# Second-layer projections of a two-layer streaming encoder: the two value products moved among the query products, the sink terms loaded earlier

## The chip, the cores and the metric

The kernel runs on one core of one Trainium2 chip. The metric is the device time of one execution in microseconds (us), given as the median of several runs. The engines are named as in the profile: PE (TensorE), DVE (VectorE), ACT (ScalarE), POOL (GpSimd) and SP (SyncE, whose queue issues all the DMAs of this kernel).

## The reference, cut to what matters

One step of a hybrid encoder on a prompt of 4096 tokens and a sample of 64 tokens, model width 1024. Layer 0 is a gated convolution module. Keys and values come from one shared projection behind it, and layer 1 reads them in a windowed attention with one learned sink per head.

```python
def trunk(x, conv_hist, k_prefix, v_prefix):
    ...
    x, h = conformer_conv_layer(x, conv_hist[i], a_pre_g[i], ...)   # layer 0
    kv = rmsnorm(x, kv_g) @ w_kv                  # 1024 x 256: keys | values
    ...
    x = swa_layer(x, ctx, b_pre_g[j], b_w_in[j], b_sinks[j], b_w_out[j], b_post_g[j])

def swa_layer(x, ctx, pre_g, w_in, sinks, w_out, post_g):
    h = rmsnorm(x, pre_g)
    z = h @ w_in                                  # 1024 x 2048: query | gate
    q, gate = jnp.split(z, 2, axis=-1)
    o = sink_alibi_attention(q, kb, vb, q_pos, k_pos, sinks)
    y = (o * jax.nn.silu(gate)) @ w_out
    return x + rmsnorm(y, post_g)

def sink_alibi_attention(q, k, v, q_pos, k_pos, sinks):
    ...
    sink = sinks.reshape(N_KV_HEADS, GROUP)[None, None, :, :, None, None]
    m = jnp.maximum(jnp.max(s, axis=-1, keepdims=True), sink)
    p = jnp.exp(s - m)
    denom = jnp.sum(p, axis=-1, keepdims=True) + jnp.exp(sink - m)
```

## The kernel before

The program has three stages in the order of time: layer 0 (0 to some 1550 us of the trace), the second layer's projections (some 1550 to 1996 us), and attention with gate and output projection (to the end at 2940 us). The change touches a load that belongs to the third stage and the order of work in the second.

**The projection stage** goes through 16 blocks of 256 prompt tokens, and through the sample. A block has two tiles of 128 tokens. `load_x1` (L1038 to L1048) reads the rows of layer 0 back from DRAM, four DMAs of 128 KB per tile (L1046), two tiles ahead of their use. `prep_x1` normalises: per tile four ACT squares with sums (L1063), one matmul `tot` that adds them over partitions (L1068), a reciprocal root (DVE L1070, POOL L1073), four scaled copies into PSUM (ACT L1085, `pst_b`), four DVE transposes (L1089), and the split of the result in two fp16 halves, `hTb` (ACT L1091 high, DVE L1092 low). From both tiles come the sums that a Strassen product needs, `tf` (POOL L1119 to L1127), split in the same way into `tTb` (ACT L1103, DVE L1104). `hTb` and `tTb` are stored to DRAM (L1135, L1137) for the gate of the third stage.

`proj_qkv` (L1170 to L1260) lists the products of one block. Each full product is three fp16 passes. The query projection is one level of Strassen (L990 to L1032): seven products p1, p5, p6, p2, p7, p4, p3, each 48 matmuls (L983), into three PSUM tiles: `sx_q` holds p1, p6, p7 and p4 in turn and is copied out by ACT between them (L1001, `P_q`, `U_q`), `sz_q` holds p5 and then p3, `sw_q` holds p2. Behind p7, DVE adds `sz_q` into the copied tile (L1256, `U_q<-sz_q,U_q`), and p3 goes on in the same `sz_q`, so p3 has to wait for that add. `k_job` is one key product (`psk`, 24 matmuls, L189 to L191), `v_job(0)` and `v_job(1)` are the value products of the two tiles (`psv`, 24 matmuls each), drained by ACT (L1185) and DVE (L1186) into `vo`. Queries are drained likewise (ACT L1231, DVE L1232, `q`).

`sz_q` and both `psv` come from one PSUM pool of two buffers. `sz_q` is held from p5 to the end of p3's drain, so while a block is between p5 and p3 its two value products share the one other buffer: the second waits until the first is drained.

**What sets the order.** The code appends work as closures, and a scheduler fixes each engine's instruction order when the program is built, from its own estimate of times. The list that `proj_qkv` returns (L1260) is what the change rewrites; the order on all engines around it follows from it. In eight of the blocks a step of preparing the gate's weights runs as well (`strassen_chunk`, L924 to L975: eight loads `wst` at L934, ACT L943, POOL L953, casts L960 and L961); these are called gated blocks here, the others plain blocks. Gated blocks fill some 1657 to 1874 us.

**The sink terms.** `sk` (L1375 to L1378) holds the 16 sinks on all partitions: two DMAs that each write 64 partitions times 8 elements of 4 bytes, from a rearranged source that is repeated over the partitions. `nsk` (eight DVE multiplies, L1382) and `unsc` (eight POOL memsets, L1383) are made from it or beside it, and the attention reads them after 2000 us. In this order of the program `sk` is loaded behind the convolution weights' close (`main_w.close()`), at the start of the projection stage.

Of the kernel before, what the change touches and what calls it, by code (L numbers as in the profile page):

```python
# [12 lines left out]
F32 = mybir.dt.float32  # L13
# [5 lines left out]
P = 128  # L19
# [48 lines left out]
def tile_streaming_conformer(  # L68
# [5 lines left out]
    nc = tc.nc  # L74
# [8 lines left out]
    cpool = ctx.enter_context(tc.tile_pool(name="const", bufs=1))  # L83
# [9 lines left out]
    def ps_cv(shape, name):  # L93
        return pcv["pool"].tile(shape, F32, tag="cv", name=name)
# [82 lines left out]
    def mm3(out, wts, mov, low_last=False):  # L177
        n = len(wts)
        if low_last:
            for i in range(n):  # L180
                nc.tensor.matmul(out, wts[i][0], mov[i][0], start=i == 0, stop=False)  # L181
                nc.tensor.matmul(out, wts[i][0], mov[i][1], start=False, stop=False)  # L182
            for i in range(n):
                nc.tensor.matmul(out, wts[i][1], mov[i][0], start=False, stop=i == n - 1)  # L184
            return
        for i in range(n):
            wh, wl = wts[i]
            mh, ml = mov[i]
            nc.tensor.matmul(out, wh, mh, start=i == 0, stop=False)  # L189
            nc.tensor.matmul(out, wh, ml, start=False, stop=False)  # L190
            nc.tensor.matmul(out, wl, mh, start=False, stop=i == n - 1)  # L191
# [27 lines left out]
    def big(shape, dt, name):  # L219
        return wk.tile(shape, dt, tag="big", name=name, bufs=6)  # L220
# [687 lines left out]
    for g in range(1, 4):  # L908
        nc.gpsimd.tensor_copy(fv[:, g], fv[:, 0])

    gq = cpool.tile([P, 4, KB], F32, name="gq")
    for j in range(4):
        nc.gpsimd.tensor_scalar(gq[:, j], gsc[:, 2], scalar1=2.0**j, scalar2=None, op0=ALU.mult)
# [76 lines left out]
    def strassen(w, h, t, tmp, out, nm):  # L990
        def bl(kh, th):
            return lambda z, kb: h[z][:, KH * kh + kb, th * P : th * P + P]

        def tl(x):
            return lambda z, kb: t[z][:, x, kb, :]

        X = {}

        def cp(name, src):
            X[name] = tmp(f"{name}_{nm}", name)  # L1000
            nc.scalar.copy(X[name], src)  # L1001

        def p1():
            X["X"] = ps_mm([P, KH, P], f"sx_{nm}")
            sprod(X["X"], w["A11"], bl(0, 0), True, False)
            cp("P1", X["X"])

        def p5():
            X["Z"] = ps_cz([P, KH, P], f"sz_{nm}")
            sprod(X["Z"], w["S1"], tl(0), True, False)  # L1010

        def p6():
            sprod(X["X"], w["S2"], tl(1), False, False)
            cp("U2", X["X"])

        def p2():
            X["W"] = ps_mm([P, KH, P], f"sw_{nm}")
            sprod(X["W"], w["A12"], bl(1, 0), True, True)
            out(0, 0, X["W"], X["P1"])

        def p7():
            sprod(X["X"], w["S3"], tl(2), False, False)
            cp("U3", X["X"])
            out(1, 1, X["Z"], X["U3"])

        def p4():
            sprod(X["X"], w["A22"], tl(3), False, True)
            out(1, 0, X["X"], None)

        def p3():  # L1030
            sprod(X["Z"], w["S4"], bl(1, 1), False, True)
            out(0, 1, X["Z"], X["U2"])  # L1032

        return [p1, p5, p6, p2, p7, p4, p3]
# [135 lines left out]
    def proj_qkv(b, ht, pool):  # L1170
# [12 lines left out]
        def put_v(src, n, scale, dst, name):  # L1183
            o = pool.tile([P, 2, P], F16, tag="vo", name=name)
            nc.scalar.activation(o[:n, 0], src, AF.Copy, scale=scale)  # L1185
            nc.vector.scalar_tensor_tensor(  # L1186
                out=o[:n, 1], in0=src, scalar=scale, in1=o[:n, 0], op0=ALU.mult, op1=ALU.subtract
            )
            nc.sync.dma_start(out=dst, in_=o[:n])
# [16 lines left out]
        def v_job(i):  # L1206
            n = min(P, T - i * P)
            last = samp or t0 + i * P + n == SEQ
            ps = ps_cv([P, 2 * P], f"psv_{b}_{i}")
            wts = [(hT[0][:, kb, i * P : i * P + n], hT[1][:, kb, i * P : i * P + n]) for kb in range(KB)]  # L1210
            lo = 0 if last else P
            mv = [(w_kv.at(0, kb, lo, 2 * P - lo), w_kv.at(1, kb, lo, 2 * P - lo)) for kb in range(KB)]
            mm3(ps[:n, lo : 2 * P], wts, mv)
            put_v(ps[:n, P:], n, SX / SP, v_scs[WIN:] if samp else v_scr[t0 + i * P : t0 + i * P + n], f"vo_{b}_{i}")
            if last:
                kv = big([P, D], F32, f"kvo_{b}")
                nc.scalar.activation(kv[:n, : 2 * P], ps[:n], AF.Copy, scale=1.0 / SP)
                for c, dst in ((0, ck_s if samp else ck_p), (P, cvv_s if samp else cvv_p)):
                    nc.sync.dma_start(
                        out=dst[0, WIN - n : WIN].rearrange("t k d -> t (k d)"), in_=kv[:n, c : c + P]  # L1220
                    )
# [35 lines left out]
            put_q(nh, th, src)  # L1257

        q = strassen(wq, hT, tT, tmp, out, f"q{b}")
        return [q[0], q[1], k_job, q[2], q[3], q[4], lambda: v_job(0), q[5], lambda: v_job(1), q[6]]  # L1260

    hts = {}
    with ExitStack() as ph:
# [48 lines left out]
    stp = ctx.enter_context(tc.tile_pool(name="stp", bufs=1))  # L1312
# [59 lines left out]

    bias = stp.tile([P, 3 * CH], F32, tag="bias", name="bias", bufs=1)
    nc.sync.dma_start(out=bias, in_=ins["alibi"])
    sk = stp.tile([P, 2, 4], F32, tag="sk", name="sk", bufs=1)  # L1375
    sinks = ins["b_sinks"][0].rearrange("(a t s) -> s a t", a=2, s=2)
    for s_ in range(2):
        nc.sync.dma_start(out=sk[s_ * 64 : s_ * 64 + 64], in_=sinks[s_].partition_broadcast(64))  # L1378
    nsk = stp.tile([P, 2, 4], F32, tag="nsk", name="nsk", bufs=1)
    unsc = stp.tile([P, 2, 4], F32, tag="unsc", name="unsc", bufs=1)  # L1380
    for t in range(8):
        nc.vector.tensor_scalar_mul(nsk[:, t // 4, t % 4 : t % 4 + 1], sk[:, t // 4, t % 4 : t % 4 + 1], -SQ * 2.0**t)  # L1382
        nc.gpsimd.memset(unsc[:, t // 4, t % 4 : t % 4 + 1], 2.0**-t / SQ)  # L1383
# [54 lines left out]
    with ExitStack() as ph:  # L1438
# [29 lines left out]
        for q_, b in enumerate(order3):  # L1468
            jobs = deque(proj_qkv(b, hts[b], p3))
            if q_ > 0 and q_ + 1 < nb:  # L1470
                b2 = order3[q_ + 1]
                hts[b2], steps = prep_x1(b2, x1n.pop(0))
                nxt.extend(steps)
            n = max(1, len(jobs))
            per = -(-len(nxt) // n)
            while jobs:
                jobs.popleft()()
                for _ in range(per):
                    if nxt:
                        nxt.popleft()()  # L1480
            while nxt:
                nxt.popleft()()
            if q_ + 2 < nb:
                x1n.append(load_x1(order3[q_ + 2]))
            while wnext:
                with queued():
                    wnext.pop()()
            for js, at in ((ojobs, 0), (gjobs, G_AT)):
                if js and q_ >= at:
                    load, comp = js.popleft()  # L1490
                    load()
                    wnext.append(comp)
            if q_ == nb - 2:
                load_att(0)
                gate_load(0)
# [315 lines left out]
```

## Time and profile before

| | us |
|---|---|
| median of 3 runs | 2932.94 |
| range of the runs | 2931.07 to 2938.25 |
| the profiled execution | 2942.24 |
| its span, first to last instruction | 2940.2 |
| PE busy in the span | 2777.6 |
| DVE busy in the span | 2263.9 |
| a plain block (1632.04 to 1656.89) | 24.85 |
| gated blocks, mean of eight (1656.89 to 1873.82) | 27.1 |

The profiled execution is 9.3 us above the median of the runs, and 2.0 us of its time lie outside the span. An engine's busy time is the sum of its instructions' durations. A row of a timeline gives an instruction's start, its duration, the engine, the line and the tiles, and in brackets how long the engine had been idle before it and what released it. A block's time is counted here from the second value product of one block to that of the next.

### The profile page before, as it was taken

What the parts mean: (1) busy time and instruction counts of PE and PEld (TensorE: products, weight loads), DVE (VectorE), ACT (ScalarE), POOL (GpSimd) and SP (SyncE); (2) the same over time, 40 slices, a digit from 0 to 9 for tenths busy, and PEclk for the clock granted to TensorE, in tenths of its full rate; (3) what the DMA queues carried; (4) which work ended last, traced back from release to release, by engine and by line L of the source; (5) the groups of instructions that cost most, each with busy time, mean ns of one, the idle gap of its engine ahead of it and who ended that gap; (6) DMA issues with size and microseconds to landing.
All of it is one profiled execution on the core that took longest, in us unless ns stands there. A gap on an engine that the chain in (4) does not pass through costs nothing. (4 is left out here: it accounts for less than half of the span.)

```text
span 2940.2 us, 62260 instructions
## 1 busy us (share of the span) xinstructions
PE 2777.6 (94%) x24441; PEld 1803.0 (61%) x24441; DVE 2263.9 (77%) x3828; ACT 1785.4 (61%) x3957; POOL 1689.9 (57%) x1614
## 2 busy tenths in 40 slices
PE   7988999999999997989998999998999999999998
PEld 5433454444444443444448999997777777777775
DVE  5899888989888889978885777754667766666665
ACT  5666667666765565556675777743565565556554
POOL 4888578779876798887752343323333343433432
PEclk9999999999999998999999999999999999999999
DMA  5121111121120124656655656666233422332321
GB/s 165 55 79 68 52 54 49 38 71 44 50 74 34 39 70 133 204 170 199 190 181 173 218 201 214 220 210 203 78 101 95 145 93 93 118 123 84 113 79 60
DMA packets 256011, 341.16 MB, mean 116 GB/s; under 512 B 40070, under 2 KB 184198, under 8 KB 254950
## 3 DMA queue, kind: packets, MB, share of 16 engines
q1 hardware_dynamic: 255717, 337.20, 35.7%
q8 instruction: 191, 3.13, 0.4%
q14 instruction: 103, 0.84, 0.1%
HBM read 206.46 MB, written 130.72 MB: 115 GB/s over the span
## 5 line engine op out<-in xcount | busy, mean ns | idle before, releaser
L622 DVE SCALAR_TENSOR_TENSOR acc<-u,pt,acc 128x1024 f32<-128x1024 f32 x608 | 782.3, 1287 | 63.7 <-ACT acc L615 49.7
L606 POOL TENSOR_TENSOR pacc<-pacc,prods 128x1024 f32<-128x1024 f32 x213 | 506.2, 2378 | 114.9 <-ACT prods L597 82.3
L597 ACT ACTIVATE prods<-u,pt 128x1024 f32<-128x1024 f32 x213 | 242.2, 1145 | 95.2 <-POOL pacc L606 94.4
L1567 ACT ACTIVATE p<-p,st 128x192 f32<-128x192 f32 (+1 forms) x520 | 228.8, 443 | 90.9 <-DVE st L1561 86.5
L606 POOL TENSOR_TENSOR pacc<-pacc,pr 128x1024 f32<-128x1024 f32 x107 | 254.4, 2378 | 39.6 <-ACT pr L597 34.7
L1540 DVE CUSTOM_DVE_ANT_0 p<-sc,bias 128x192 f32<-128x192 f32 (+1 forms) x520 | 159.6, 350 | 82.0 <-PE sc L1537 59.4
L1586 POOL TENSOR_TENSOR p<-p,st 128x768 f32<-128x768 f32 (+2 forms) x130 | 189.8, 1480 | 37.9 <-DVE st L1582 35.8
L181 PE MATMUL psy<-w_oa,hl 128*128 128x512 f16 x512 | 199.4, 389 | 10.5 <-ACT hl L307 9.2
L189 PE MATMUL ps_gt<-hT,w_gt 128*128 128x512 f16 x512 | 196.0, 383 | 10.1 <-ACT w_gt L160 5.2
L182 PE MATMUL psy<-w_oa,hl 128*128 128x512 f16 x512 | 198.8, 388 | 3.3 <-DVE w_oa L161 3.3
L189 PE MATMUL ps_a<-hT,w_a 128*128 128x512 f16 (+1 forms) x528 | 198.6, 376 | 3.0 <-ACT sig L785 1.9
L191 PE MATMUL ps_a<-hT,w_a 128*128 128x512 f16 (+1 forms) x528 | 198.4, 376 | 3.2 <-DVE w_a L161 3.1
L189 PE MATMUL ps_gl<-hT,w_gl 128*128 128x512 f16 (+1 forms) x528 | 198.4, 376 | 1.9 <-ACT sig L785 1.2
L181 PE MATMUL psy<-w_ob,ogT 128*128 128x512 f16 x512 | 194.1, 379 | 5.0 <-ACT ogT L1652 5.0
L190 PE MATMUL ps_gl<-hT,w_gl 128*128 128x512 f16 (+1 forms) x528 | 197.7, 375 | 0.8 <-DVE hT L208 0.8
L190 PE MATMUL ps_a<-hT,w_a 128*128 128x512 f16 (+1 forms) x528 | 198.4, 376 | 0.0
L191 PE MATMUL ps_gl<-hT,w_gl 128*128 128x512 f16 (+1 forms) x528 | 197.9, 375 | 0.0
L191 PE MATMUL ps_gt<-hT,w_gt 128*128 128x512 f16 x512 | 195.2, 382 | 2.7 <-DVE w_gt L161 2.7
L190 PE MATMUL ps_gt<-hT,w_gt 128*128 128x512 f16 x512 | 196.1, 383 | 0.0
L182 PE MATMUL psy<-w_ob,ogT 128*128 128x512 f16 x512 | 194.1, 379 | 0.0
L983 PEld LDWEIGHTS <-w_qS 128*128 128x128 f16 x3072 | 180.1, 100 | 11.3 <-issue 10.9
L983 PEld LDWEIGHTS <-w_gS 128*128 128x128 f16 x3072 | 180.5, 98 | 8.7 <-issue 6.9
(363 smaller groups left out, 7171.7 us busy)
## 6 DMA issues: line engine op xcount, KB each, us to landing
x<-in_x_prompt SPq DMA_DIRECT2D x32, 512.0 KB, 3.4
g_scr<-sg SPq DMA_DIRECT2D x64, 256.0 KB, 2.0
c_scr<-c SPq DMA_DIRECT2D x32, 512.0 KB, 2.6
c<-c_scr SPq DMA_DIRECT2D x32, 512.0 KB, 5.7
g<-g_scr SPq DMA_DIRECT2D x32, 512.0 KB, 4.3
x<-x_scr SPq DMA_DIRECT2D x128, 128.0 KB, 3.7
h_scr<-hTb SPq DMA_DIRECT2D x32, 512.0 KB, 3.4
h_scr<-tTb SPq DMA_DIRECT2D x32, 512.0 KB, 4.8
```

What stands on the lines that cost most here:

```text
L181: nc.tensor.matmul(out, wts[i][0], mov[i][0], start=i == 0, stop=False)
L182: nc.tensor.matmul(out, wts[i][0], mov[i][1], start=False, stop=False)
L189: nc.tensor.matmul(out, wh, mh, start=i == 0, stop=False)
L190: nc.tensor.matmul(out, wh, ml, start=False, stop=False)
L191: nc.tensor.matmul(out, wl, mh, start=False, stop=i == n - 1)
L597: nc.scalar.activation(dst[:, :T], u[:, k : k + T], AF.Identity, scale=wdw[:, j, k : k + 1], bias=pt[:, j, R_DWB : R_DWB + 1] if k == 0 el ...
L606: nc.gpsimd.tensor_tensor(out=pacc[:, :T], in0=pacc[:, :T], in1=dst[:, :T], op=ALU.add)
L622: nc.vector.scalar_tensor_tensor(out=acc[:, :T], in0=u[:, k : k + T], scalar=wdw[:, j, k : k + 1], in1=acc[:, :T], op0=ALU.mult, op1=ALU.add,)
L983: nc.tensor.matmul(ps[:, j, :], w[:, wz, kb, j * P : j * P + P], rhs(rz, kb), start=first and j + kb + wz + rz == 0, stop=last and j == KH ...
L1540: nc.vector.tensor_tensor_reduce(out=pbuf[:, t, par * 192 + lo : par * 192 + 192], in0=ps[:, tt, :nk], in1=bias[:, lo:], scale=1.0, scalar ...
L1567: nc.scalar.activation(pp, pp, AF.Exp, scale=2.0 ** -(kv * 4 + t) / SQ, bias=st[:, 1, par, t : t + 1], accum_out=st[:, 3, par, t : t + 1],)
L1586: nc.gpsimd.tensor_tensor(out=pp, in0=pp, in1=st[:, 4, par, :, None].to_broadcast([P, 4, 3 * CH - lo]), op=ALU.mult)
```

## The change

The list of `proj_qkv` is reordered: the two value products, which stood behind p7 and p4, now stand behind p1 and behind p6, with the key product between them. The tile `sk` moves to the pool of constants and its two DMAs are issued in the code of the setup ahead of layer 0; `nsk` and `unsc` move to the same pool.

```diff
@@ -908,6 +908,10 @@
+    sk = cpool.tile([P, 2, 4], F32, name="sk")
+    sinks = ins["b_sinks"][0].rearrange("(a t s) -> s a t", a=2, s=2)
+    for s_ in range(2):
+        nc.sync.dma_start(out=sk[s_ * 64 : s_ * 64 + 64], in_=sinks[s_].partition_broadcast(64))
@@ -1257,7 +1261,7 @@
         q = strassen(wq, hT, tT, tmp, out, f"q{b}")
-        return [q[0], q[1], k_job, q[2], q[3], q[4], lambda: v_job(0), q[5], lambda: v_job(1), q[6]]
+        return [q[0], lambda: v_job(0), q[1], k_job, q[2], lambda: v_job(1), q[3], q[4], q[5], q[6]]
@@ -1372,12 +1376,8 @@
-    sk = stp.tile([P, 2, 4], F32, tag="sk", name="sk", bufs=1)
-    sinks = ins["b_sinks"][0].rearrange("(a t s) -> s a t", a=2, s=2)
-    for s_ in range(2):
-        nc.sync.dma_start(out=sk[s_ * 64 : s_ * 64 + 64], in_=sinks[s_].partition_broadcast(64))
-    nsk = stp.tile([P, 2, 4], F32, tag="nsk", name="nsk", bufs=1)
-    unsc = stp.tile([P, 2, 4], F32, tag="unsc", name="unsc", bufs=1)
+    nsk = cpool.tile([P, 2, 4], F32, name="nsk")
+    unsc = cpool.tile([P, 2, 4], F32, name="unsc")
```

Where the scheduler puts the sink loads: SP's queue at the very start of the program, after. `x_...<-in_x_prompt` are the first eight tiles of the prompt, `wst<-in_a_w_in` weights of layer 0.

```order
L462 DMA x_3_321<-in_x_prompt 128x1024
L914 DMA sk<-in_b_sinks 64x8x1 x2
L1706 DMA out<-in_cache_k 16x512
L1706 DMA out<-in_cache_v 16x512
L150 DMA wst<-in_a_w_in 128x8x128
L504 DMA rows<-in_a_b_in 3x1024
```

Before, the same rows stand without `sk`, so the two loads were put directly behind the eight tiles of the prompt and ahead of the third weight load. On DVE the eight multiplies that read `sk` stand, after, in the first weights of layer 0:

```order
L473 TENSOR_SCALAR x_3_197<-x_3_197,r_3_239 128x1024
L1382 TENSOR_SCALAR nsk<-sk 128x1 x8
L161 SCALAR_TENSOR_TENSOR w_gl_83<-wst,gsc,w_gl_83 128x128 x2
```

They moved there from the start of the projection stage. Up to that stage all other instructions of the five engines keep their order.

In the gated block of the queries `q_6`, PE before runs the second value product behind p4 (`sx_q` from `w_qA`), and p3 (`sz_q`) behind it:

```order
L983 MATMUL sx_q_16357<-tTb_0_15773,w_qA_10261 128x128
L189 LDWEIGHTS hTb_0_15771
L189 MATMUL psv_1_16796<-w_kv,hTb_0_15771 128x128
...
L191 MATMUL psv_1_16796<-w_kv,hTb_1_15772 128x128
L983 LDWEIGHTS w_qS_10262
L983 MATMUL sz_q_16418<-hTb_0_15771,w_qS_10262 128x128
```

After, the same product stands behind p6 (`sx_q` from `w_qS`) and ahead of p2 (`sw_q`):

```order
L987 MATMUL sx_q_16357<-tTb_0_15773,w_qS_10261 128x128
L189 LDWEIGHTS hTb_0_15771
L189 MATMUL psv_1_16606<-w_kv,hTb_0_15771 128x128
...
L191 MATMUL psv_1_16606<-w_kv,hTb_1_15772 128x128
L987 LDWEIGHTS w_qA_10262
L987 MATMUL sw_q_16642<-hTb_0_15771,w_qA_10262 128x128
```

The second value product moved ahead by three query products (p2, p7, p4), and p3 follows p4 directly. The first value product went to the end of p1 of its block; there PE, after, runs the sums of the next block's first tile (`tot_0`) in front of it:

```order
L987 MATMUL sx_q_16939<-hTb_0_16353,w_qA_10259 128x128
L1072 MATMUL tot_0_16995<-ssqx_0_16990,fold 128x4
L189 LDWEIGHTS hTb_0_16353
L189 MATMUL psv_0_17000<-w_kv,hTb_0_16353 128x128
```

Before, p5 (`sz_q_17000`) stood behind this `tot_0`; what moved is the product behind it, 24 matmuls of `psv` that now lie between `tot_0` and the key product and p5.

SP's queue in the same gated block, before: the stores of `hTb` (two halves) stand among the loads of a later block's `x`.

```order
L1046 DMA x_8_0_16882<-x_scr 32x4x256
L1135 DMA h_scr<-hTb_0_16353 128x2048
L1046 DMA x_8_0_16882<-x_scr 32x4x256 x2
L1135 DMA h_scr<-hTb_1_16354 128x2048
L1046 DMA x_8_0_16882<-x_scr 32x4x256
L1046 DMA x_8_1_16887<-x_scr 32x4x256
L1189 DMA v_scr<-vo_0_16718 128x256
```

And after:

```order
L1193 DMA v_scr<-vo_1_16631 128x256
L1139 DMA h_scr<-hTb_0_16353 128x2048
L1139 DMA h_scr<-hTb_1_16354 128x2048
L1050 DMA x_8_0_16882<-x_scr 32x4x256 x4
L1050 DMA x_8_1_16887<-x_scr 32x4x256 x4
L1141 DMA h_scr<-tTb_0_16355 128x2048
```

All eight loads of `x_8` now stand behind the store of the second half, `hTb_1`, which DVE finishes; before, three of the first tile's four stood ahead of it.

DVE in that stretch, before:

```order
L1232 SCALAR_TENSOR_TENSOR q_6_0_16621<-sw_q_16570,q_6_0_16620 128x512
L1092 TENSOR_TENSOR hTb_1_16354<-x_7_1_16305,hTb_0_16353 128x8x64 x2
L1256 TENSOR_TENSOR U_q_16679<-sz_q_16418,U_q_16679 128x512
L1104 TENSOR_TENSOR tTb_1_16356<-tf_0_16722,tTb_0_16355 128x4x64 x2
L1186 SCALAR_TENSOR_TENSOR vo_0_16718<-psv_0_16693,vo_0_16718 128x128
L1232 SCALAR_TENSOR_TENSOR q_6_1_16683<-U_q_16679,q_6_1_16682 128x512
```

And after:

```order
L1260 TENSOR_TENSOR sw_q_16642<-sw_q_16642,P_q_16406 128x512
L1096 TENSOR_TENSOR hTb_1_16354<-x_7_1_16305,hTb_0_16353 128x8x64 x2
L1236 SCALAR_TENSOR_TENSOR q_6_0_16693<-sw_q_16642,q_6_0_16692 128x512
L1108 TENSOR_TENSOR tTb_1_16356<-tf_0_16696,tTb_0_16355 128x4x64 x2
L1260 TENSOR_TENSOR U_q_16755<-sz_q_16454,U_q_16755 128x512
L1108 TENSOR_TENSOR tTb_1_16356<-tf_1_16762,tTb_0_16355 128x4x64 x2
```

The drain of the value product left this stretch (it stands earlier, with `vo_1` ahead of the transposes), and the add of `sz_q` into `U_q`, for which p3 waits, moved behind a query drain and two `tTb` steps. In the third stage the scheduler interleaves the same instructions in a slightly different order throughout.

## Rows read from the trace of the kernel before

**Rows 1.** Page: busy time and share of PE; shares of the chain that ended last.

```profile
PE 2777.6 (94%) x24441; PEld 1803.0 (61%) x24441; DVE 2263.9 (77%) x3828; ACT 1785.4 (61%) x3957; POOL 1689.9 (57%) x1614
...
PE 25%; DVE 2%; ACT 2%; issue 0%; POOL 0%; POOLq 0%; ACTq 0%; DVEq 0%
```

**Rows 2.** By stage: stretch, length, busy of each engine, PE clock, DMA, GB/s.

```profile
1632.00:1657.00 25.00, 24.71 (x414) 24.32 (x414) 17.11 (x34) 17.06 (x48) 8.23 (x7) 1.00 0.59 204
1657.00:1874.00 217.00, 201.81 (x3300) 198.57 (x3299) 165.65 (x321) 159.59 (x451) 92.51 (x81) 0.98 0.63 213
...
2100.00:2940.00 840.00, 819.23 (x9033) 617.54 (x9030) 555.20 (x1656) 469.89 (x1510) 303.48 (x498) 1.00 0.33 102
```

**Rows 3.** Waits of PE, 1556 to 2000: total us, times, longest.

```profile
PE psv L189 <- DVE vo L1186: 16.4, 13, 2.6
PE sx_q L983 <- ACT U_q L1001: 9.4, 1, 9.4
```

**Rows 4.** Timeline from 1556: the sink loads and what starts behind them.

```profile
1557.94 1.35 SPq L1378 DMA_DIRECT2D sk<-in_b_sinks  x2
...
1558.14 2.84 PE L983 MATMUL sx_q<-tTb,w_qS 128*128 128x128 f16 x48 [0.18 <-ACT P_q L1001]
...
1560.62 5.92 SPq L934 DMA_DIRECT2D wst<-in_b_w_in  x5
...
1570.07 0.58 DVE L1382 TENSOR_SCALAR nsk<-sk 128x1 f32<-128x1 f32 x8 [11.23 <-DMA wst<-in_b_w_in]
...
1572.52 2.72 PE L983 MATMUL sx_q<-tTb,w_qS 128*128 128x128 f16 x24 [9.36 <-ACT U_q L1001]
```

**Rows 5.** DMA, 1557 to 1571: rate in 40 slices of 0.35 us, and packets.

```profile
GB/s 0 0 0 0 105 176 0 0 0 0 0 0 0 0 0 0 0 0 0 0 0 0 0 0 0 0 0 0 1 0 3 62 113 176 201 280 348 268 208 196
DMA packets 1918, 0.75 MB, mean 54 GB/s; under 512 B 1164, under 2 KB 1789, under 8 KB 1917
```

**Rows 6.** By stage as in rows 2: the PE clock around that stop.

```profile
1565.00:1570.00 5.00, 0.00 (x0) 0.00 (x0) 0.00 (x0) 0.00 (x0) 0.00 (x0) 0.67 0.29 86
1570.00:1575.00 5.00, 2.48 (x24) 2.48 (x24) 4.60 (x16) 2.33 (x5) 2.92 (x2) 0.50 0.68 208
```

**Rows 7.** Timelines of the start: SP's loads, then the first waits for weights.

```profile
3.65 5.74 SPq L462 DMA_DIRECT2D x<-in_x_prompt  x5
...
12.34 0.39 SPq L150 DMA_DIRECT2D wst<-in_a_w_in  x1
...
27.73 2.42 POOL L158 TENSOR_SCALAR w_a<-wst,gsc 128x128 f16<-128x128 f32 x4 [3.26 <-DMA wst<-in_a_w_in]
...
29.48 1.11 PE L206 MATMUL pst_a<-ident,x 128*128 128x128 f32 x4 [2.33 <-DVE hT L208]
```

**Rows 8.** DMA, 2 to 20, then rate of 18 to 34 in 0.4-us slices.

```profile
DMA packets 4355, 5.89 MB, mean 327 GB/s; under 512 B 212, under 2 KB 3284, under 8 KB 4355
...
GB/s 113 77 74 64 79 215 127 125 298 332 317 188 31 146 271 346 379 192 23 18 22 22 23 23 26 23 28 0 0 0 0 0 41 0 110 159 300 335 289 64
```

**Rows 9.** Timelines of one gated block, engine by engine.

```profile
1806.95 0.34 PE L1068 MATMUL tot<-ssqx,fold 128*128 128x4 f32 x2
...
1819.09 0.22 PE L189 MATMUL psv<-w_kv,hTb 128*128 128x128 f16 x1 [1.90 <-DVE vo L1186]
...
1825.29 0.34 PE L1068 MATMUL tot<-ssqx,fold 128*128 128x4 f32 x2
...
1812.94 3.07 DVE L1092 TENSOR_TENSOR hTb<-x,hTb 128x512 f16<-128x512 f32 x2
...
1816.54 2.30 DVE L1104 TENSOR_TENSOR tTb<-tf,tTb 128x256 f16<-128x256 f32 x2
...
1821.99 0.42 ACT L1063 ACTIVATE hTb<-x 128x256 f16<-128x256 f32 x1 [2.20 <-DMA v_scr<-vo]
...
1817.48 1.45 SPq L1046 DMA_DIRECT2D x<-x_scr  x2
```

**Rows 10.** By stage, PE alone: a stretch with a long wait of the second value product.

```profile
1760.00:1770.00 10.00, 7.37 (x106) 0.83 0.87 292
```

## The prediction

> **What bounds the kernel now.** I read the page first, then the table by stage, then the waits of PE in the stage that the change rewrites, and last the timelines at the places found. PE is busy for 94% of the span, and the chain that ended last runs through PE more than through any other engine [rows 1]. So a change is worth what it takes from PE's idle time and PE's clock. In the projection stage two waits of PE stand out [rows 3]: 16.4 us in 13 pieces, where a second value product waits until DVE has drained the first, and one piece of 9.4 us ahead of `sx_q`. In the plain block of 25 us PE idles for 0.3 us; in the 217 us of the eight gated blocks it idles for 15.2 us [rows 2]. The third stage has 20.8 us of PE idle in 840 [rows 2], in many small pieces.
>
> The single wait of 9.4 us is the sink loads' doing [rows 4]. SP issues both at 1557.94, each element a packet of its own: 1164 of the 1918 packets in 1557 to 1571 are under 512 B, and 1024 of them are `sk` (2 x 64 partitions x 8). From 1559.1 to 1567.5, 24 slices of 0.35 us, the DMA engines move nothing else [rows 5], though weights are issued from 1560.62 on. DVE stands at `nsk` until 1570.07, 11.23 us; the transposes are queued behind it, ACT's `hTb` casts behind those, and the copy `U_q` behind these, for which PE waits until 1572.52. The profile names a weight load as the releaser of `nsk`, but that wait is for `sk`, which `nsk` reads.
>
> **The sink terms, taken away.** 9.36 us of PE wait go. The clock falls with it: 0.67 and 0.50 are granted in the two stretches behind [rows 6], 0.50 being the lower of the two levels (1.2 of 2.4 GHz). At that clock 24 matmuls took 2.72 us where 48 take 2.84 at full clock [rows 4], so 1.3 us are lost on this half product, and on the rest until the clock is back about 0.7, which I estimate. Sum **-11.4**. Bounds -8 and -11.4: with `nsk` gone DVE meets the transposes when ACT's `pst_b` is done, and nothing that PE needs there is due later.
>
> **The sink terms, put at the start.** The orders show that the loads land not one stage ahead of their use but at the very start, behind the eight loads of the prompt and ahead of the third weight load, and that `nsk` stands on DVE ahead of layer 0's next weights. Two queues are passed. SP has issued the prompt by 9.4 us and issues the third weight load at 12.34 [rows 7]. The transfers are busy there: 5.89 MB in 2 to 20 us at a mean of 327 GB/s [rows 8]; eight tiles and two weight loads are 5.24 MB, so the prompt's data lasts to about 16 us. Behind it come weights that are waited for: POOL and DVE idle for `w_a` until 27.73, and PE waits behind that at 29.48 [rows 7]. Up to there the last load trails at 18 to 28 GB/s, from 25.2 to 28.8 us [rows 8], so nothing is spare in this chain, and a later load is a later start of everything behind it, since the order up to the second stage is otherwise the same. How long is it later? If the small packets wait their turn behind the prompt's data and then block as they did at 1559, it is the whole 8.4 us. If they are worked off from their issue at 9.4 us on, while the prompt's data still flows until 16, 6.6 of the 8.4 are hidden and 1.8 are left. No row decides; the stop at 1559 had idle engines and only shows that what is issued behind the sinks doesn't pass them. I take **+5.0**, the middle, and keep +1.8 and +8.4. `nsk` itself is 0.58 us on an idle DVE, the eight memsets 0.30 on POOL, both hidden in waits for loads.
>
> The Trainium skill, page "DMA: Bandwidth & Descriptors", section "Queues, rings and completion order", says that each DMA engine takes an issuing queue's descriptors in ring order. The stop agrees so far as nothing issued behind the sinks passed them. By that rule, with the small packets behind all of the prompt's data, the start would cost its upper end, which is the third case below.
>
> **The value products.** After, the second value product follows the first by three quarters of the key product, p5 and p6, some 8 us of PE work, while its drain is two operations of 0.3 us; its wait for the drain goes, 16.4 us in all [rows 3]. For the plain blocks this is 0.25 us each in five of the 13 pieces, **-1.0** with bounds 0 and -1.2.
>
> In the gated blocks another wait takes its place. What ends last is a loop through the next tile's sums. PE's own work in a block is seven products of 2.68, two value products of 1.34, the key product of 2.62 and the two `tot`, 24.5 us; the eight gated blocks take 27.1 on average. In the traced block [rows 9] the second tile's `tot` starts at 1806.95 and the second tile's `hTb` is split at 1812.94 + 3.07 = 1816.0, 9.1 later. The fourth load of a later tile is issued at 1817.48 and ACT's squares of that tile start at 1821.99, 4.5 later, having waited 2.20 for it. (The row names a value store; a load of `x` is what the squares read.) The squares take 1.7, then comes `tot`, here asked for only at 1825.29 and not waited for. After the change, three things move in this loop:
> - All four loads stand behind the store of the split `hTb`. One store is 0.4 and a load 0.73 (two in 1.45), so the fourth is issued 0.4 + 3 x 0.73 = 2.6 after the split and not 1.5. `tot` can start 2.6 + 4.5 + 1.7 + 0.1 = 8.9 after the split.
> - From that `tot` to the second tile's `tot` PE has a value product (1.34), three quarters of the key product (1.97), p5 (2.68), the rest of the key product (0.65) and 35 matmuls of p6 (1.96): 8.6.
> - From there to the split 9.1 as before, or 0.5 less because the `sw_q` add left the place ahead of the transposes: 8.8.
>
> One round is 8.9 + 8.6 + 8.8 = 26.3 us, 1.8 more than PE's work, so PE now idles about 1.8 at `tot` where it idled 1.6 to 2.6 at the value product. The add into `U_q` stands behind a query drain and two `tTb` steps (0.65 and 2.30) and ends some 3.6 behind the split, about when PE comes to p3, so p3 waits little or nothing. Of the clock: three of the eight gated blocks had a stretch at 0.83 as in [rows 10], 3.4 us at the lower level and so 1.7 lost each; with waits as long I leave 0.6 per block in. 26.3 + 0.6 against 27.1 is -0.2 a block, within what I can read; I take **0** for the eight. Bounds: without any new wait 8 x (24.5 - 27.1) = -21; with the loads landing 1.5 later, for which this stage's 0.63 DMA share leaves room, +12 with the clock's share.
>
> **The third stage** runs the same work in another interleaving: 0, with +-5 as a bound, a quarter of its 20.8 us of idle either way.
>
> Sum: -11.4 + 5.0 - 1.0 + 0 = **-7.4**. Against the profiled execution that is 2942.2 - 7.4 = 2934.8. The profiled execution lies 9.3 above the median of the runs, so on the runs' scale 2932.9 - 7.4 = 2925.5, rounded to **2926**.
>
> **Rivals.**
> - *The loop doesn't bind* (faster). For it: the loads' 4.5 us were taken beside weight loads, and after the change the eight stand in a row; if they land sooner, or the chain to the split gets shorter once DVE has one drain less in it, `tot` is ready when asked. Against it: SP's order, which puts all of them behind the split. Then -11.4 + 5.0 - 1.0 and up to -21 in the gated blocks; with two thirds of that -21.4: **2911**.
> - *The new wait is longer than the old one* (slower). Place: `tot` of the first tile in each gated block, and p3 behind the `U_q` add. 1.5 us later loads make a round 27.8, a clock dip in every block 29.5, against 27.1: 8 x 2.4 = +19; with the sum's other terms +12.6: **2945**. It decides from a round of about 28.0 on, where it eats the -7.4; for it speaks that DMA is busier in a gated block than in a plain one (0.63 against 0.59 [rows 2]) and that waits of the value product reached 2.6 already.
> - *The start pays in full*: -11.4 + 8.4 - 1.0 = -4.0: **2929**, by the ring order of the skill's page. Weighed against it: the small packets' issue comes 6.6 us before the prompt's data ends.
> - *The stop is not the sinks'*: then nothing goes at 1560 and only the start costs, -1 + 5: 2937. Against it: the rate of zero for 8.4 us and the count of small packets.
>
> **Chances.** Forecast 0.34, loop doesn't bind 0.27, start in full 0.17, longer wait 0.18, not the sinks' 0.04. About 0.3% (8.8 us) is what a measurement of this kernel can tell from no change, so below 2924 is faster and above 2942 slower. The forecast lies close to the lower bound, so a third of it counts as faster: faster 0.27 + 0.12 = 0.39, same 0.43, slower 0.18. The range reaches from 2909 (most of the case in which the loop doesn't bind) to 2944 (about half of the longer wait).
>
> **What would show it.** Right: no stop of PE around 1560 to 1572 and no half clock there; `nsk` early on DVE, the first `w_a` on POOL some 5 us later than 27.7, with PE's matmuls of layer 0 all shifted by as much until 1550; no waits of `psv` on `vo`; instead waits of `tot` for the ACT squares, about 1.8 us in each gated block, and a gated block of 26 to 27 us. Wrong: a start shift under 2 or over 8; gated blocks of 25 us, or of 28 and more with clock dips in each; a wait of p3 on the `U_q` add of more than 1 us; over 5 us of change in the third stage.

## The result and the profile after

The changed kernel takes 2954.04 us (median of five runs, 2951.67 to 2963.69) where the kernel before takes 2932.94: 1.0070 times the time, 95% interval 1.0058 to 1.0081, some 20 us slower. The prediction was 2926 with a range of 2909 to 2944, so it is wrong in sign and outside its range.

The two profiled executions alone show less, 2949.3 against 2940.2 us of span, because the first profiled execution of the kernel before lay 9.3 above its median. A second profile of it (run r_before below) has 2936.4; what follows is set against that one, and rows of the first are named by their group. Set so, the traced pair differs by 12.9 us. The medians differ by 18.5 (from r_before's 2935.52) to 21.1; the traced run of before lies 3.2 above its median and that of the changed kernel 1.8 below, and no trace shows the rest.

PE's busy time is unchanged to the tenth [rows 1]; only idle time was added. The page after:

```profile
PE 2777.6 (94%) x24441; PEld 1798.7 (61%) x24441; DVE 2269.8 (77%) x3828; ACT 1780.6 (60%) x3957; POOL 1690.7 (57%) x1614
```

The waits of PE from 1540 to 2010 us (total us, times, longest) answer to [rows 3]:

```profile
PE tot L1072 <- ACT hTb L1067: 23.0, 9, 3.6
PE sx_q L987 <- ACT U_q L1005: 4.7, 6, 1.1
PE sz_q L987 <- DVE U_q L1260: 4.3, 5, 0.9
PE sz_q L987 <- DVE tTb L1108: 2.8, 1, 2.8
```

Both waits of [rows 3] are gone, the 16.4 us of `psv` and the single 9.4. In their place `tot` waits 23.0 us for the ACT squares, longer than `psv` did, and p3 waits for the add into `U_q` (third row). By stage (stretch, length, busy of each engine with counts, PE clock, DMA share, GB/s), a plain block and the gated blocks:

```profile
1646.00:1671.00 25.00, 24.34 (x411) 23.95 (x409) 18.74 (x36) 17.41 (x52) 10.62 (x10) 1.00 0.53 175
1671.00:1900.00 229.00, 204.23 (x3295) 197.90 (x3293) 163.71 (x317) 157.68 (x444) 89.84 (x77) 0.97 0.65 204
```

The eight gated blocks take 229 us where they took 217 [rows 2], though PE has the same matmuls in them (3295 and 3300 recorded).

The start, as SP, DVE and POOL show it in their timelines (start, duration, what, and the idle time before it with its releaser):

```profile
8.45 1.42 SPq L914 DMA_DIRECT2D sk<-in_b_sinks  x2
...
25.36 0.58 DVE L1382 TENSOR_SCALAR nsk<-sk 128x1 f32<-128x1 f32 x8 [8.18 <-DMA sk<-in_b_sinks]
...
27.21 2.35 POOL L158 TENSOR_SCALAR w_gl<-wst,gsc 128x128 f16<-128x128 f32 x4 [6.86 <-DMA wst<-in_a_w_in]
...
34.91 2.42 POOL L158 TENSOR_SCALAR w_a<-wst,gsc 128x128 f16<-128x128 f32 x4 [5.08 <-DMA wst<-in_a_w_in]
```

`w_a`, at 27.73 in [rows 7], starts 7.2 us later. To see where the rest went I counted, at each mark, the matmul work that the second profile of before had done, and took the time at which another run had done as much; a figure is that run's lateness in us. The runs of the second to the last column are told below. The first profile of before, counted the same way, stands at +2.1, +2.7, +2.1, +0.6, 0.0 and +3.8, so a difference of 2 to 4 us between two columns can be chance.

```
mark in r_before   after  e1_list  e2_sink  e3_xearly  f1_row  f3_v0_row_early
1540 (layer 0 done) +5.3    0.0     +5.0      +7.4      +0.7       +1.5
1580 (behind stop)  -4.7   +0.5     -5.8      -2.7      -7.9       -6.4
1640                -1.2   +3.6     -2.1      -4.1      -8.0       -8.3
1900 (gated done)  +10.3  +16.9     -4.3     -14.1     -11.5      -23.5
2000               +12.1  +20.3     -4.7     -11.6     -11.8      -24.7
end                +12.9  +21.1     -3.2     -10.2     -11.2      -23.2
```

The column of after: 5.3 lost at the start, 10.0 gained at the stop, 3.5 lost in the blocks right behind it, 11.5 in the gated blocks, 1.8 in the last blocks and the sample, and next to nothing in the third stage.

### The profile page after: what moved, and what is told of

It reads as the page before. It is cut to its first block, busy times and chain, and to the rows that moved or that the text cites. A ratio compares the mean times of both kernels' runs of the same rounds, so it can differ in the third digit from the quotient of the medians.

```text
span 2949.3 us, 62242 instructions
## 1 busy us (share of the span) xinstructions
PE 2777.6 (94%) x24441; PEld 1798.7 (61%) x24441; DVE 2269.8 (77%) x3828; ACT 1780.6 (60%) x3957; POOL 1690.7 (57%) x1614
```

## The experiments

Ratios are against the kernel before, run on the same chip beside each kernel (median 2934.8 to 2936.9).

### The two halves of the change

**e1_list** changes the list alone:

```diff
-        return [q[0], q[1], k_job, q[2], q[3], q[4], lambda: v_job(0), q[5], lambda: v_job(1), q[6]]
+        return [q[0], lambda: v_job(0), q[1], k_job, q[2], lambda: v_job(1), q[3], q[4], q[5], q[6]]
```

> The list of products alone, sinks loaded where they were before. Theory A, read from the two traces: the list costs, by the new wait of the first tile's tot for the ACT squares (23.0 us in 9 pieces) in place of 16.4 us of psv; the stop at 1560 stays. Then slower than before by 18 to 30 us, gated blocks of 28 to 29 us as in the changed kernel. Theory B, the loads at the start are the larger cost: then this one is slower by at most 13 us.

Measured: 2956.87, ratio 1.0076 (1.0063 to 1.0089), 22 us slower. The whole loss is the list's. Its gated blocks, by stage, have the lowest clock of all runs, 0.95:

```profile
1676.00:1907.00 231.00, 208.92 (x3300) 201.49 (x3298) 164.35 (x319) 157.83 (x445) 89.44 (x77) 0.95 0.62 203
```

**e2_sink** moves the sinks alone to the start, with the list as before:

```diff
+    sk = cpool.tile([P, 2, 4], F32, name="sk")
+    for s_ in range(2):
+        nc.sync.dma_start(out=sk[s_ * 64 : s_ * 64 + 64], in_=sinks[s_].partition_broadcast(64))
...
-    sk = stp.tile([P, 2, 4], F32, tag="sk", name="sk", bufs=1)
...
```

> The sinks alone at the start, list as before. Theory A: the stop of 11.4 us at 1560 goes and the start costs 3 to 8, so faster than before by 3 to 9 us; PE's first matmuls behind the weights some 7.5 us later, gated blocks as before (27 us), psv waits of 16 us as before. Theory B: the start costs more than the stop gave, slower by up to 8 us.

Measured: 2936.01, ratio 1.0005 (0.9996 to 1.0014): no change. By the table the start costs 5.0 and the stop gives 10.8 back, but at the second block `tot` waits 3.3 us, where the second profile of before has 1.2. The waits, e2_sink first (the `psv` row from 1540 to 2010) and r_before second:

```profile
PE psv L189 <- DVE vo L1190: 18.0, 13, 2.6
PE tot L1072 <- ACT hTb L1067: 3.3, 1, 3.3
```

```profile
PE psv L189 <- DVE vo L1186: 16.9, 13, 2.6
PE sx_q L983 <- ACT U_q L1001: 9.9, 2, 9.4
PE tot L1068 <- ACT hTb L1063: 1.2, 1, 1.2
```

SP has its own backlog of loads for the attention in that stretch (`ks`, and before it `v` and `qraw`). It issued the first of the next `x` loads at 1597.30, 2.8 us behind the split of `hTb` (1593.36 + 1.16), and ACT's squares waited for them:

```profile
1594.64 2.55 SPq L1426 DMA_DIRECT2D ks<-k_scr  x4
1597.30 1.99 SPq L1050 DMA_DIRECT2D x<-x_scr  x2
...
1605.47 0.42 ACT L1067 ACTIVATE hTb<-x 128x256 f16<-128x256 f32 x1 [5.75 <-DMA x<-x_scr]
```

So the time that PE had gained was in part waited away again.

**r_before** is the kernel before, unchanged.

> The kernel before, unchanged, for a second profile of it: the first profiled execution lay 9 us above the median of the runs. Expected: ratio 1.000 within 0.002; where the profiled execution lies at 2931 to 2935, its stages show which of them was long in the first profile; if the first profile's stages repeat, the offset belongs to profiling.

Measured: 2935.52, ratio 1.0003 (0.9995 to 1.0012), and its profiled execution at 2938.7. It lies 3.2 above its median and not 9.3; the first profile's span is another 3.8 us longer, in small pieces: 2.1 in layer 0, made up by 2000, and 3.8 in the third stage.

### What makes tot late

The code puts the `x` loads of the block after next at the end of a block. **e3_xearly** is the changed kernel with them at its beginning; PE, DVE and POOL keep their order.

```diff
+            if q_ + 2 < nb:
+                x1n.append(load_x1(order3[q_ + 2]))
             jobs = deque(proj_qkv(b, hts[b], p3))
...
-            if q_ + 2 < nb:
-                x1n.append(load_x1(order3[q_ + 2]))
```

> The changed kernel, with each block's x loads put into the code one block earlier; PE, DVE and POOL keep their order, SP issues the loads of a tile a whole block ahead of the squares that read it. Theory A (the loop through the loads binds the gated blocks): the waits of tot go from 23 us to under 4, gated blocks fall from 28.9 to 25 to 26 us, and the kernel is 20 to 28 us faster than the changed one, so 0 to 8 faster than before. Rival C, the squares are late for ACT's own queue or the split chain and not for the loads: gated blocks stay above 28 and the time stays within 5 us of the changed kernel's.

Measured: 2928.88, ratio 0.9976 (0.9966 to 0.9987), 25 us faster than the changed kernel and 6 faster than before, as theory A had it. PE's waits in its gated blocks:

```profile
PE sz_q L987 <- DVE U_q L1260: 7.0, 8, 0.9
PE tot L1072 <- ACT hTb L1067: 2.3, 8, 0.3
```

Up to the end of the gated blocks only SP's order changed (nine ACT instructions change places behind them, at 1947 to 1954), and the waits of `tot` went from 20.1 us in the eight gated blocks to 2.3. So it was the loads. Every gated block now takes 25.97 us, of which 0.9 is p3's wait.

**f5_before_early** is the same edit on the kernel before.

> The kernel before with only the x loads put one block earlier in the code. Theory A, in the list before the loads don't bind and the second value product's wait for the drain does: psv waits of 14 to 18 us stay, the time is before's within 5 us. Rival, the loads bind in both lists: 8 to 20 us faster than before.

Measured: 2927.19, ratio 0.9976 (0.9966 to 0.9987), 7.6 us faster by the medians, between the two expectations. Of the 16.9 us that `psv` waited in r_before most stay, 1.6 in every gated block, and the longest is 1.6 where it was 2.6:

```profile
PE psv L189 <- DVE vo L1186: 14.1, 13, 1.6
```

What went are the longer ones of these waits and the clock's falls behind them: the gated blocks take 26.2 us each, without exception, where r_before has three of eight at 28.4 to 29.5 (from `tot` to `tot`). That points to late loads in the long blocks of the list before, and not behind the 1.6 us of the others. By which path they lengthened a wait is not shown, and besides SP's order some of DVE's and ACT's changed here too. The granted clock is 1.00 and no longer 0.98 [rows 2]:

```profile
1671.00:1880.00 209.00, 196.10 (x3288) 192.97 (x3286) 164.16 (x316) 154.39 (x441) 89.03 (x76) 1.00 0.67 222
```

**f2_v0** takes half of the list: the first value product as in the change, the second where it was.

```diff
-        return [q[0], q[1], k_job, q[2], q[3], q[4], lambda: v_job(0), q[5], lambda: v_job(1), q[6]]
+        return [q[0], lambda: v_job(0), q[1], k_job, q[2], q[3], q[4], q[5], lambda: v_job(1), q[6]]
```

> Half of the new list: the first value product behind p1 as in the change, the second left ahead of p4, sinks and all else as before. SP's order here has two of a tile's four x loads behind the store of the split hTb, PE the second value product between p7 and p4. Theory A, SP's order makes the wait: the psv waits go, tot waits 0.5 to 1.5 us in a gated block and p3 not at all, gated blocks 25.5 to 26.5 us, 3 to 12 us faster than before. Rival, it is the earlier first value product that makes tot late whatever SP does: gated blocks of 28 us or more, 10 to 20 us slower.

Measured: 2936.93, ratio 1.0009 (1.0000 to 1.0019), so neither expectation: the waits moved and their sum stayed, and the gated blocks take 26.9 us each in the mean. SP has two of four loads ahead of the store of the second half here, and `tot` waits 3.9 us in the gated blocks, between the 20.1 of the full list and the 2.3 with early loads; but p3 now waits 11.4 us for the `U_q` add, which I had expected at zero:

```profile
PE sz_q L983 <- DVE U_q L1256: 11.4, 8, 1.5
PE tot L1068 <- ACT hTb L1063: 3.9, 5, 1.6
```

### The sinks, and the versions put together

**f1_row** leaves the sinks at their old place and loads them as one row of 16 neighbouring elements:

```diff
-    sinks = ins["b_sinks"][0].rearrange("(a t s) -> s a t", a=2, s=2)
+    skr = stp.tile([P, 16], F32, tag="skr", name="skr", bufs=1)
+    nc.sync.dma_start(out=skr, in_=ins["b_sinks"][0].partition_broadcast(P))
     for s_ in range(2):
-        nc.sync.dma_start(out=sk[s_ * 64 : s_ * 64 + 64], in_=sinks[s_].partition_broadcast(64))
+        h = slice(s_ * 64, s_ * 64 + 64)
+        nc.vector.tensor_copy(sk[h], skr[h].rearrange("p (a t s) -> p s a t", a=2, s=2)[:, s_])
```

> The kernel before with the sinks loaded at their old place, but as one row of 16 neighbouring elements repeated over the partitions (128 packets of 64 bytes for 1024 of 4) and spread by two DVE copies. Theory A, the stop at 1560 is the 1024 element packets: PE's wait of 9.4 us goes and no start is paid, but a wait of tot of some 3.5 us at 1608 takes its place as in the run with the sinks at the start; 5 to 9 us faster than before. Rival: the broadcast load or the weight load named by the profile is slow by itself; then nsk still waits 8 us or more and the time is before's within 3 us.

Measured: 2926.37, ratio 0.9968 (0.9956 to 0.9980), 8.4 us faster by the medians. The wait for the sinks shrank from 11.23 [rows 4] to 2.09 us, on DVE:

```profile
1559.65 0.35 DVE L1380 COPY sk<-skr 64x8 f32<-64x8 f32 x2 [2.09 <-DMA skr<-in_b_sinks]
1560.03 0.58 DVE L1384 TENSOR_SCALAR nsk<-sk 128x1 f32<-128x1 f32 x8
```

The wait of `tot` that I expected at 1608 did not come: it is 1.2 us, as in r_before. The stop gave less, 8.6 by the table (from +0.7 to -7.9) and not 10.8, and all of it was kept up to 1640.

**g1_twice** loads the sinks twice at the start, into two tiles of which one is read, with the list before.

```diff
+    sk2 = cpool.tile([P, 2, 4], F32, name="sk2")
+    for s_ in range(2):
+        nc.sync.dma_start(out=sk2[s_ * 64 : s_ * 64 + 64], in_=sinks[s_].partition_broadcast(64))
```

> The list before; the sinks loaded at the start twice, into two tiles (four DMAs, 2048 element packets), only one read. For the price of the start, in the profile: with one load nsk waited until 25.2 us and PE ran 5 us late. Theory A, the first load is hidden behind the prompt's data for about half of its 9.6 us and a second is hidden behind nothing: nsk unchanged within 1 us, the third weight load and all behind it another 8.4 to 9.6 us later, PE some 14 us late in layer 0. Rival, the packets cost a share each (5 us per load): PE some 10 us late.

Measured once: 2945.43, PE 14.5 us late in layer 0 where one load makes it 5.0. DVE, then POOL:

```profile
26.37 0.57 DVE L1385 TENSOR_SCALAR nsk<-sk 128x1 f32<-128x1 f32 x8 [8.43 <-DMA sk<-in_b_sinks]
```

```profile
36.72 2.41 POOL L158 TENSOR_SCALAR w_gl<-wst,gsc 128x128 f16<-128x128 f32 x4 [15.24 <-DMA wst<-in_a_w_in]
```

The DMA rate from 2 to 42 us, in 40 slices of 1 us, first with one load (e2_sink), then with two:

```profile
GB/s 262 377 375 282 348 375 337 324 381 411 401 401 422 414 120 13 0 12 44 42 47 98 181 188 188 228 318 224 246 61 19 22 14 0 16 83 338 110 2 0
```

```profile
GB/s 242 377 381 295 343 376 353 400 411 427 418 422 422 312 50 17 0 0 0 0 0 0 0 0 0 0 0 3 24 39 64 111 241 193 192 266 328 297 108 30
```

The price of a second load is 9.5 us in full, as theory A had it, but its reason for the smaller price of the first does not hold: the packets are not worked off beside the prompt's data. The count of small packets shows it. From 9 to 16 us, while that data flows, r_before (first) and e2_sink (second) have the same 80; from 16 to 25.2 us they have 115 and 1116:

```profile
DMA packets 1183, 2.74 MB, mean 392 GB/s; under 512 B 80, under 2 KB 575, under 8 KB 1183
DMA packets 1191, 2.76 MB, mean 394 GB/s; under 512 B 80, under 2 KB 581, under 8 KB 1191
...
DMA packets 2709, 1.97 MB, mean 215 GB/s; under 512 B 115, under 2 KB 2579, under 8 KB 2709
DMA packets 1867, 0.60 MB, mean 65 GB/s; under 512 B 1116, under 2 KB 1791, under 8 KB 1867
```

So the sinks' packets begin when the prompt's data ends and take some 9 us. What makes one load cheaper than that is behind it: from 20 us on weights move beside the last of the packets (44, 42, 47, 98 and 181 GB/s in the first rate row), and `w_gl` starts on POOL at 27.08, 6.6 us later than in r_before (20.46), `w_a` 6.0 later, PE 5.0. Where the last 1.6 us of these are made up is not shown. With two loads nothing moves until 29 us, and this tail comes once.

**f3_v0_row_early** puts together the half list, the row and the early loads.

> The same half of the list, the sinks as one row, and the x loads put one block earlier in the code. Theory A: neither tot nor psv nor p3 is waited for, gated blocks of 24.7 to 25.3 us (16 to 19 us for eight), the stop gone (10.8 us) and no wait at 1608: 24 to 32 us faster than before. Rival, what binds the gated blocks behind the loads is DVE or the DMA share: gated blocks stay at 26 or more, 10 to 18 us faster.

Measured: 2914.87, ratio 0.9931 (0.9916 to 0.9946), 20 us faster than before by the medians, between the two expectations. **g2_list_row_early** has the full list instead of its half.

> The full new list with the sinks as one row at their old place and the x loads one block earlier: what the changed list is worth when neither its loads nor the sinks are in the way. Theory A: as the changed kernel with early loads (6 us faster than before), without the 5 us at the start: 9 to 13 us faster than before, gated blocks 25.97 with 0.9 of wait at p3; the half list stays ahead by some 5 to 8 us because its sample and last blocks don't stretch (26 for 37 us there). Rival, the list is as good as its half: 18 to 22 us faster than before.

Measured: 2921.18, ratio 0.9945 (0.9928 to 0.9962), 15.8 us faster by the medians, between the two expectations; the interval is too wide to set it apart from f3 on the ratio alone. In the gated blocks of f3 no wait of `tot` or `psv` is left:

```profile
1662.00:1866.00 204.00, 197.16 (x3306) 194.06 (x3304) 158.82 (x316) 157.17 (x444) 88.63 (x77) 1.00 0.70 229
...
1800.30 2.84 PE L983 MATMUL sz_q<-hTb,w_qS 128*128 128x128 f16 x48 [0.86 <-DVE U_q L1256]
```

They take 25.5 us each; what remains above PE's 24.5 is p3's 0.86 and small gaps. My expectation of 24.7 to 25.3 was too low by that wait.

## Why the prediction was wrong

Of the 20.3 us between the forecast of -7.4 and the traced +12.9, 11.5 are the gated blocks, 6.3 the blocks around them (the 1.0 that the plain blocks were to give included), 1.4 the stop, 0.8 the third stage and 0.3 the start.

**The sinks at the start: right in size, by luck.** +5.0 was taken between 1.8 and 8.4, and e2_sink shows +5.0 at the end of layer 0. The reason given for the middle was only that no row decided. The lower end had the packets worked off beside the prompt's data, and they were not: e2_sink has no more small packets from 9 to 16 us than r_before. The Trainium skill, page "DMA: Bandwidth & Descriptors", section "Queues, rings and completion order", says that descriptors are consumed in ring order on each engine. The counts agree with it. So the third rival, "the start pays in full", had the order right and the price wrong: it took 8.4, with "nothing is spare in this chain", and 3.4 us of that were spare behind the packets.

**The sinks taken away: the stop went, its worth was too high.** It gave 10.8 and not 11.4 by 1580 us, but the sentence that "nothing that PE needs there is due later" failed. SP's queue was due: with the stop gone, the loads of the next `x` came late behind the attention's loads, and `tot` waited 3.3 us. So e2_sink has -7.1 (from +5.0 to -2.1, up to 1640) where the sum has -11.4, and f1_row, without that wait, -8.7. With +5.0 that leaves -2.1 in the profile, and in the medians of the runs no change, where the prediction had -6.4.

**The value products: the mechanism was right, its price was not.** The waits of `psv` went, and the loop through the first tile's `tot` bound in their place. The step that failed is the sum of that loop, 26.3 us: it measures 28.1 in the four rounds in which the loads stand behind the store and the clock does not fall, and 28.7 in the mean of the eight. One round of it after the change, at 1805, as the timelines have it:

```profile
1805.34 0.39 PE L1072 MATMUL tot<-ssqx,fold 128*128 128x4 f32 x2 [3.60 <-ACT hTb L1067]
...
1814.17 0.34 PE L1072 MATMUL tot<-ssqx,fold 128*128 128x4 f32 x2
...
1820.79 3.08 DVE L1096 TENSOR_TENSOR hTb<-x,hTb 128x512 f16<-128x512 f32 x2
...
1822.70 1.52 SPq L1139 DMA_DIRECT2D h_scr<-hTb  x2
1824.27 5.29 SPq L1050 DMA_DIRECT2D x<-x_scr  x8
...
1831.52 0.42 ACT L1067 ACTIVATE hTb<-x 128x256 f16<-128x256 f32 x1 [2.34 <-DMA x<-x_scr]
...
1827.35 2.84 PE L987 MATMUL sz_q<-hTb,w_qS 128*128 128x128 f16 x48 [0.87 <-DVE U_q L1260]
...
1833.75 0.39 PE L1072 MATMUL tot<-ssqx,fold 128*128 128x4 f32 x2 [2.73 <-ACT hTb L1067]
```

And all eight, term by term, from the same instructions:

```
                                   predicted  before   after (8 gated blocks)
tot of tile 0 to tot of tile 1        8.6       8.2    8.8 in five, 10.5, 11.6 and 10.5 in three
to the split's end                    8.8       9.1    9.7 in five, 8.9 to 9.0 in the same three
to the issue of the fourth load       2.6       1.5    2.5 to 3.9 in seven, 0.4 in the last
to the squares                        4.5       4.5    4.0 to 5.3
to tot                                1.8       1.7    2.2
round                                26.3              28.1 28.3 27.7 29.9 31.3 28.4 29.6 26.0
```

(The before column is the traced block of [rows 9]; its last term is the squares' own time, since PE came to `tot` later than that.) In the four rounds with loads behind the store and no fall of the clock (28.1, 28.3, 27.7 and 28.4) each term was low in the mean, the split by 0.9, the others by 0.1 to 0.4, 1.8 in all. The 0.5 taken off the split for the `sw_q` add was wrong: DVE does that add just ahead of the split now (1820.21 to 1820.88), in the place of the query drain that had left it, which the printed order already showed. ACT's squares were cut by a query drain, 2.2 for 1.7. Of the loads in a row the second and the third take 1.1 and 1.3 us to issue in this round, where [rows 9] has two in 1.45. In the last gated block three of the four loads stand ahead of the store of the second half, and its round is 26.0 with a wait of 0.3. Such a loop takes the sum of all its small errors eight times. The clock's part comes on top: in three of the eight rounds it fell in the products behind `tot`, which then took 1.7 to 2.7 us longer to the second `tot`, while the split took 0.7 less. That is some 0.5 a block, and the 0.6 in the sum was about right. 0.83 was granted in the stretch behind the wait of 1833.75:

```profile
1830.00:1840.00 10.00, 7.27 (x82) 0.83 0.72 245
```

The mean round is 28.7 against 27.1 before: +1.6 a block, some 13 us (11.5 in the table, against r_before), where I took 0. The rival "the new wait is longer than the old one" named the place and the point from which it decides (28.0); it was given 0.18 with 2945. (With the sum's other terms its +19.2 makes +11.8, and not the +12.6 written there.)

**What was not in the sum.** The plain blocks got no better: p4 has no value product between p7 and itself any more and waits some 0.7 us for the copy `U_q` (the second row of the waits after), which I had not priced. Behind the stop the second block has a wait of `tot` of 2.9 us and a lower clock. The last block and the sample cost 1.8 us in the changed kernel and 3.4 in e1_list, between 1900 and 2000, where PE waits 2.8 us for `tTb` (the fourth row). The third stage was forecast at 0 within 5 and is 0.8.

**The chances** rested on a loop whose margin to the old time was 0.2 us a block. A term known to 0.5 in each of five places cannot carry "0 for the eight"; the bound of +12 was there, and +11.5 to 13 came.

## What to carry to other kernels

A wait removed from a loop is worth its length less what the next-longest loop leaves, so sum that loop from rows, term by term, and take its uncertainty times the number of rounds; here five terms that were each a little low made some +12 us of a forecast 0. Look at the DMA queue as an engine with an order of its own: here loads put behind a store that waits for DVE inherited that wait, and moving the loads ahead by a block brought back 25 us without touching any computation. A small broadcast load of single elements is better loaded as a contiguous row and spread on chip (8.4 us here) than moved to another place, where its packets block whatever comes next (no gain here). And a forecast that hits between two bounds is no evidence for either mechanism: count the packets.

## What the runs showed of the hardware

Single-element packets are dear for what is issued behind them and cost nothing to what is issued ahead: 1024 packets of 4 bytes held up everything behind them for 8.4 us at 1559 [rows 5] and for 9.5 us in g1_twice, while the prompt's loads issued ahead of them kept their rate of 280 to 430 GB/s, and the small packets began only when these ended. Twice the bytes, 64 per partition in one run of 16 elements, let DVE wait 2.09 us. The Trainium skill, page "DMA: Bandwidth & Descriptors", section "Rules for kernel authors", has the rule that a last dimension which isn't contiguous lowers to one descriptor per element; the count of small packets agrees.

The clock took part in the waits. Gated blocks with waits of 1.6 us at one place kept 1.00 (f5_before_early, 26.2 us each). Behind the seven waits of 2.0 to 3.6 us after the change it fell three times, to 0.66 to 0.83 in stretches of 10 us, and each fall made the stretch to the second `tot` 1.7 to 2.7 us longer. The length of the wait alone did not decide: the longest, 3.60 at 1805, and one of 3.03 kept 1.00, and one of 2.04 did not.
